# A decoder layer on one core: sums of tokens in portions one step apart, the first weight sums by DMA asked for later, and one load over ScalarE's queue

## The chip, the cores and the metric

The kernel runs on one core of one Trainium2 chip. The metric is the device time of one execution in microseconds (us). The kernel before took 818.30 us (median of three runs, 817.43 to 819.27).

## What is computed

One layer of a hybrid decoder on 256 tokens of width 2048, all in float32. Cut to what matters here:

```python
h = rmsnorm(x, norm_mix_g)
u = h @ w_in                       # 16384 columns: ten fields, the last two are ga and gb, 2048 wide each
ya = b_g * causal_dwconv3(c_g * xa) * silu(za)
yb = hgrn2(q, f, iv) normed per head * silu(og)
m = sigmoid(ga) * (ya @ w_a_out) + sigmoid(gb) * (yb @ w_b_out)
x = x + m @ w_o
x = x + sigmoid(rmsnorm(x) @ w_ple_gate) * (p @ w_ple_proj)
out = rmsnorm(x, final_norm_g)
```

## The kernel before

**One product in three.** Every float32 operand is cut into a high part, rounded to the type float32r, and the rest. A product is three matmuls, high by high, high by low and low by high (`triple`, L1030 to L1034); each has 128 tokens on the partitions and 512 columns. `cut` (L163) makes the two parts of a weight tile: ScalarE (ACT) copies to the high part (`whi`, L164) and VectorE (DVE) subtracts it (`wlo`, L165).

**Items and the loop.** The weights are walked in a list of items, one turn of the main loop (L1096) each. An item brings 256 rows by 512 columns: 1024 elements on each partition, 12 matmuls. At turn `pos` the loop cuts the item that lies three ahead (`ahead`, L1026) into one of four pairs of buffers, so its `whi` waits until TensorE has finished the item that used the pair before. Raw weights come over SyncE's queue (SP) in 1 MB loads of two items into three buffers.

**The part around the change.** `begun` is the last item of the gate ga of column group 0. I count from it and write b+1, b+2 and so on. b+1 to b+8 are gb of group 0, b+9 to b+12 `w_a` ("A0"), b+13 to b+16 `w_b` ("B0"). From b+17 on group 1 computes ga and gb together by a scheme of seven products in the place of eight, over tiles of 128 tokens by 128 rows. Its items are of two kinds: S items (slices c = 0, 2, 3, 5, 6) make seven products, 21 matmuls, named P1, c00, c10, P5, P7, P6, c01 in this order (`names_of`, L1049); slices 1, 4 and 7 are plain and are two C items each, 12 matmuls an item. So b+17 is S, b+18 and b+19 are C, b+20 and b+21 are S, b+22 and b+23 C, b+24 and b+25 S, b+26 and b+27 C; A1 and B1 follow. Groups 2 and 3 repeat this pattern.

**What an S item needs.** Sums of tokens: `token_sums` (L730) is a generator that makes them once, for all groups, in three portions (`TOGETHER`, L33: slice 0, slices 2 and 3, slices 5 and 6). A portion first rebuilds the tokens (`F`, in a buffer named `thi`, L744), then makes four sums (`S`, in `tlo`, L754), whose high part ACT writes to `shi` (L756) and whose low part DVE writes to `slo` (L757). Sums of weights: `add_by_dma` (L152) lets GpSimd's queue load one tile `sT` (L157) and, once that has landed, add a second one to it by an accumulating DMA (L158). `combine_weights` (L180) runs two turns ahead of the S item: two additions on DVE (L696, into `sA`) and three cuts, `sT` to `thi`/`tlo`, `sB` to `bhi`/`blo`, `sA` to `thi`/`tlo`. There are two buffers `sA` and two `sB`, loaded over SP (L141); the next load into one waits for the `tlo` or `blo` cut from it.

**What sets the order.** Generators in `active` are stepped once at the end of a turn, twice in S turns (L1174 to L1176). From `begun` to eight items past the start of A3 (`parked`) `pinned` (L1079) keeps ACT's and DVE's instructions in the order in which the code writes them; elsewhere a scheduler may reorder. TensorE's order is the scheduler's everywhere. Each engine works its queue in order, so an instruction that waits holds all behind it.

**Banks.** The products go to four PSUM banks `g` and four `s`. P6 and c01 of b+17 use the two banks that held B0's result; DVE frees them when it multiplies gb by that result (`ep_bb`, L776).

**The output projection.** O0 to O3 are `w_o`'s four column groups, eight items each. At O0's sixth item `third_part` (L996) opens the last pool and loads the first quarter of the residual x (`residual`, L983, two DMAs of 256 KB into `xs`), needed when O0 is done (`ep_o`, L816).

Of the kernel before, what the change touches and what calls it, by code (L numbers as in the profile page):

```python
# [47 lines left out]
def hybrid_kernel(ctx, tc, xT, x, pT, prm, gfin, masks, w_in, w_a, w_b, w_o, w_pg, w_pp, out):  # L48
    nc = tc.nc
# [11 lines left out]
    def open_pool(name, side):  # L61
        closers[name] = ExitStack()
        pools[name] = closers[name].enter_context(
            tc.tile_pool(name=name, bufs=1, side=side, reuse_waits="tile")
        )

    def close_pool(name):
        closers.pop(name).close()
        del pools[name]
# [3 lines left out]
    state = {"tmp": "tmp1"}  # L73
# [3 lines left out]
    def nm(s):  # L77
        uid[0] += 1
        return f"{s}_{uid[0]}"
# [5 lines left out]
    def bank(tag):  # L85
        return ps.tile([P, CW], F32, tag=tag, bufs=4, name=nm(tag))

    def sc(n, tag="sc", bufs=12):
        return small.tile([P, n], F32, tag=tag, bufs=bufs, name=nm(tag))
# [59 lines left out]
            else:  # L149
                nc.sync.dma_start(out=raw, in_=w[g, :, c : c + 2, :])  # L150

    def add_by_dma():  # L152
        pos = next((n for n, it in enumerate(items) if it["kind"] == "S" and n not in pair_sums), None)
        if pos is not None:
            w, g, c = items[pos]["w"]
            X = pair_sums[pos] = pools["st"].tile([P, 2, CW], F32, tag="sT", bufs=3, name=nm("sT"))
            nc.gpsimd.dma_start(out=X.rearrange("p n x -> p (n x)"), in_=w[g + 1, :, c, :])  # L157
            nc.gpsimd.dma_start(out=X, in_=w[g : g + 2, :, c, :CW].rearrange("n p x -> p n x"), accum_op=ALU.add)  # L158

    def pair_of(pool, n, tags=("whi", "wlo"), width=2 * CW):  # L160
        return tuple(pool.tile([P, width], F32R, tag=tag, bufs=n, name=nm(tag)) for tag in tags)
# [18 lines left out]
    def combine_weights(pos):  # L180
        st = pools["st"]
        (A, B), X = raw_of(pos), pair_sums[pos]
        add(A[:, 0], X[:, 0], B[:, 0])
        add(A[:, 1], A[:, 0], A[:, 1])
        ts = []
        for n, src in enumerate((X, B, A)):
            hi, lo = pair_of(st, 1, ("bhi", "blo"), CW) if n == 1 else pair_of(st, 3, ("thi", "tlo"))
            cut(hi, lo, src.rearrange("p n x -> p (n x)"))
            ts += [(hi[:, i * CW : (i + 1) * CW], lo[:, i * CW : (i + 1) * CW]) for i in range(1 if n == 1 else 2)]
        t1, t3, b22, t2, t4_ = ts  # L190
        sums[pos] = (b22, t1, t3, t2, t4_)
        add_by_dma()
# [4 lines left out]
    begun = next(n for n, it in enumerate(items) if it["kind"] == "ga" and it["last"])  # L197
# [532 lines left out]
    def token_sums():  # L730
        nu = len(SEVEN[1])
        state["S"] = pair_of(pools["st"], 1, ("shi", "slo"), nu * 4 * P)
        state["S"] = tuple(v.rearrange("p (u s t) -> p u s t", u=nu, s=4) for v in state["S"])
        for first, n in TOGETHER:
            for _ in range(3):
                yield
            F, S = (
                pools["st"].tile([P, 2 * CW], F32R, tag=tag, bufs=3, name=nm(tag))[:, : n * 4 * P].bitcast(F32)
                for tag in ("thi", "tlo")
            )  # L740
            c = SEVEN[1][first]
            hi, lo = (v[:, 2 * c : 2 * (c + n), :] for v in state["hT"])
            Fv = F.rearrange("p (k t) -> p k t", t=T)
            nc.vector.tensor_tensor(out=Fv, in0=hi.bitcast(F32), in1=lo.bitcast(F32), op=ALU.add)  # L744
            yield
            Fv = F.rearrange("p (u r b t) -> p u r b t", u=n, r=2, b=2)
            Sv = S.rearrange("p (u s t) -> p u s t", u=n, s=4)
            a11, a12, a21, a22 = Fv[:, :, 0, 0], Fv[:, :, 1, 0], Fv[:, :, 0, 1], Fv[:, :, 1, 1]
            s1, s2, s3, s4 = (Sv[:, :, i] for i in range(4))
            for out, u, v, op in (  # L750
                (s1, a21, a22, ALU.subtract), (s2, s1, a11, ALU.subtract),
                (s3, a11, a21, ALU.subtract), (s4, a12, s2, ALU.add),
            ):
                nc.vector.tensor_tensor(out=out, in0=u, in1=v, op=op)  # L754
            hi, lo = (v[:, first : first + n] for v in state["S"])
            nc.scalar.activation(out=hi, in_=Sv, func=AF.Copy)  # L756
            nc.vector.tensor_tensor(out=lo, in0=Sv, in1=hi.bitcast(F32), op=ALU.subtract)  # L757
            yield
# [217 lines left out]
    def second_part():  # L976

        close_pool("tmp1")
        open_pool("st", "left")
        open_pool("tmp2", "right")  # L980
        state["tmp"] = "tmp2"

    def residual(j):  # L983

        for t in range(NT):
            s = slice(j * CW, (j + 1) * CW)
            nc.sync.dma_start(out=state["x"][:, t, s], in_=x[:, t, s])

    def load_gfin():
        g = state["gfin"] = pools["tmp3"].tile([P, D], F32, name="gfin_t")  # L990
# [5 lines left out]
    def third_part():  # L996

        close_pool("tmp2")
        close_pool("branch")
        open_pool("tmp3", "right")  # L1000
        state["tmp"] = "tmp3"
        xs = pools["tmp3"].tile([P, NT, D], F32, name="xs")
        state["x"] = xs
        residual(0)
        state["ss2"] = sc(8, "ss2", 1)
        state["ss3"] = sc(12, "ss3", 1)
        nc.gpsimd.memset(state["ss3"].rearrange("p (t j) -> p t j", t=NT)[:, :, 5:6], EPS)
# [14 lines left out]
    def finish():  # L1022
        while active:
            advance()
# [71 lines left out]
    for pos, it in enumerate(items[:last_group]):  # L1096
        mark = len(nc.cur_bb.bb.instructions)
        kind, j, c, last = (it[n] for n in ("kind", "j", "c", "last"))
        _, _, w, g, opname = groups[it["gi"]]
# [60 lines left out]
        else:  # L1160
# [3 lines left out]
            for i in range(2):  # L1164
                k = 2 * c + i
                s = slice(i * CW, (i + 1) * CW)
# [10 lines left out]
        if pos == begun:  # L1177
            finish()
            second_part()
            active.append(token_sums())  # L1180
            for _ in range(3):
                add_by_dma()
        if kind == "O" and j == 0 and c == nch - 3:
            finish()
            third_part()
        if kind == "O" and j > 0 and c == 1:
            residual(j)
# [20 lines left out]
    for t, halves in ((0, (0, 1)), (1, (0,)), (1, (1,))):  # L1208
        bk, n = bank("g"), CW // 2
        for c in range(nlast):  # L1210
# [4 lines left out]
            for i in range(2):  # L1215
                k = 2 * c + i
                s = slice(i * CW + halves[0] * n, i * CW + (halves[-1] + 1) * n)
# [83 lines left out]
```

## Time and profile before

| | |
|---|---|
| median of three runs | 818.30 us |
| the profiled execution, its own time | 818.19 us |
| its span in the trace | 816.14 us |
| TensorE busy in the span | 804.2 us |
| DVE busy | 589.0 us |
| ACT busy | 459.1 us |
| mean granted TensorE clock | 0.997 |

The profile is one execution. Between its own time and the span lie 2.05 us that the trace doesn't show. All times of rows are us from the start of the span; a row of the timeline gives start, duration, engine, line, operation, tiles and, in brackets, the idle time ahead of it with what ended that. PE is TensorE. A steady stream of 512-column matmuls starts one every 0.227 us; the duration in a row (0.39) is longer because they overlap, so lost time shows in the distance between starts more than in idle time.

### The profile page before, as it was taken

The page shows a single profiled execution, that of the slowest core. Times are in us where ns is not written, and L with a number is a line of the kernel's source. Part 1 is how long each engine was busy: PE and PEld are TensorE (multiplying, and loading weights), DVE is VectorE, ACT ScalarE, POOL GpSimd, SP SyncE. Part 2 cuts the span into 40 slices and gives each one's busy share as a digit, 9 for nine tenths or more (in the row PEclk, how much of TensorE's full clock was granted, in tenths as well). Part 3 has the DMA queues.
Part 4 walks back from the last instruction along what each step waited for, and adds up shares of the span by engine and source line. Part 5 has one row for each costly group of instructions (what it writes and reads, how often), then busy time and mean ns, then how long its engine had stood idle before and what let it go on. Part 6 is the DMA issues. An engine that isn't in the chain of part 4 may idle for free.

```text
span 816.1 us, 10646 instructions
## 1 busy us (share of the span) xinstructions
PE 804.2 (99%) x4059; PEld 664.6 (81%) x4059; DVE 589.0 (72%) x745; ACT 459.1 (56%) x614; POOL 49.2 (6%) x57
## 2 busy tenths in 40 slices
PE   9999999999999999999999999999999999999995
PEld 6888888888888888888888778888888788888885
DVE  6746588767766498766778988987988756677932
ACT  7576476465555466455545556556554546575623
POOL 1000000001000000012000110110100000001210
PEclk9999999999999999999999999999999999999998
DMA  9988555647867555649975898998944887796702
GB/s 334 396 302 287 198 205 169 235 138 270 253 235 250 198 175 195 206 161 327 350 246 194 243 290 289 291 276 260 278 171 174 299 283 281 250 343 267 275 35 103
DMA packets 52659, 198.52 MB, mean 243 GB/s; under 512 B 6784, under 2 KB 16256, under 8 KB 37888
## 3 DMA queue, kind: packets, MB, share of 16 engines
q1 hardware_dynamic: 45792, 181.07, 63.1%
q0 software_dynamic: 6240, 15.73, 8.3%
q10 hardware_dynamic: 576, 1.05, 0.4%
q8 instruction: 31, 0.51, 0.3%
q14 instruction: 20, 0.16, 0.1%
HBM read 184.19 MB, written 13.63 MB: 242 GB/s over the span
## 4 chain that ended last, share of the span: by engine, by line
PE 85%; DVE 7%; issue 3%; DMA 3%; ACT 2%; POOLq 0%; POOL 0%; DVEq 0%; ACTq 0%
PE g L1033 26%; PE g L1034 26%; PE g L1032 26%; DVE wlo L165 3%; PE s L1033 2%; PE s L1034 2%; PE s L1032 2%; DMA sA<-in_w_in 1%; DMA raw<-in_w_pp 1%; DVE tlo L165 1%; ACT whi L164 1%; DMA raw<-in_w_o 1%; DVE sA L696 1%; PE s L479 1%; DVE back L303 0%
## 5 line engine op out<-in xcount | busy, mean ns | idle before, releaser
L165 DVE TENSOR_TENSOR wlo<-raw,whi 128x1024 fp32r<-128x1024 f32 (+1 forms) x264 | 319.6, 1227 | 157.9 <-ACT whi L164 155.9
L164 ACT ACTIVATE whi<-raw 128x1024 fp32r<-128x1024 f32 (+1 forms) x264 | 272.8, 1049 | 205.0 <-PE g L1034 168.8
L1033 PE MATMUL g<-wlo,xh 128*128 128x512 f32 (+1 forms) x738 | 283.9, 385 | 0.0
L1034 PE MATMUL g<-whi,xl 128*128 128x512 f32 (+1 forms) x738 | 283.6, 385 | 0.0
L1032 PE MATMUL g<-whi,xh 128*128 128x512 f32 (+1 forms) x738 | 283.5, 385 | 0.0
L1033 PEld LDWEIGHTS g<-wlo,xh 128*128 128x128 f32 x738 | 138.7, 188 | 27.7 <-DVE wlo L165 0.3
L1032 PEld LDWEIGHTS g<-whi,xh 128*128 128x128 f32 x738 | 138.7, 188 | 27.4
L1034 PEld LDWEIGHTS g<-whi,xl 128*128 128x128 f32 x738 | 138.7, 188 | 27.4
L1033 PE MATMUL g<-wlo,mh 128*128 128x512 f32 x128 | 49.9, 390 | 0.3 <-DVE wlo L165 0.3
L1032 PE MATMUL g<-whi,mh 128*128 128x512 f32 x128 | 49.7, 389 | 0.0
L1034 PE MATMUL g<-whi,ml 128*128 128x512 f32 x128 | 49.5, 389 | 0.0
L1033 PE MATMUL s<-wlo,xh 128*128 128x512 f32 x84 | 32.7, 390 | 0.0
L1034 PE MATMUL s<-whi,xl 128*128 128x512 f32 x84 | 32.7, 389 | 0.0
L1032 PE MATMUL s<-whi,xh 128*128 128x512 f32 x84 | 32.5, 390 | 0.0
L164 ACT ACTIVATE thi<-sA 128x1024 fp32r<-128x1024 f32 x15 | 15.9, 1062 | 27.6 <-DVE sA L696 24.7
L1033 PEld LDWEIGHTS g<-wlo,mh 128*128 128x128 f32 x128 | 24.0, 188 | 5.7 <-DVE wlo L165 0.7
L1032 PEld LDWEIGHTS g<-whi,mh 128*128 128x128 f32 x128 | 24.0, 188 | 5.1
L1034 PEld LDWEIGHTS g<-whi,ml 128*128 128x128 f32 x128 | 24.0, 188 | 4.9
L1034 PE MATMUL g<-whi,ybTl 128*128 128x512 f32 x64 | 24.9, 389 | 0.0
L1033 PE MATMUL g<-wlo,ybTh 128*128 128x512 f32 x64 | 24.9, 389 | 0.0
L1032 PE MATMUL g<-whi,yaTh 128*128 128x512 f32 x64 | 24.9, 389 | 0.0
L1033 PE MATMUL g<-wlo,yaTh 128*128 128x512 f32 x64 | 24.9, 389 | 0.0
(215 smaller groups left out, 908.4 us busy)
## 6 DMA issues: line engine op xcount, KB each, us to landing
raw<-in_w_in SPq DMA_DIRECT2D x66, 1024.0 KB, 5.0
raw<-in_w_o SPq DMA_DIRECT2D x16, 1024.0 KB, 6.1
raw<-in_w_pg SPq DMA_DIRECT2D x16, 1024.0 KB, 5.6
sT<-in_w_in POOLq DMA_DIRECT2D x30, 512.0 KB, 7.4
raw<-in_w_in SPq DMA_DIRECT2D x28, 512.0 KB, 6.6
raw<-in_w_a SPq DMA_DIRECT2D x8, 1024.0 KB, 6.8
raw<-in_w_b SPq DMA_DIRECT2D x8, 1024.0 KB, 6.7
turn<-t SPq DMA_DIRECT2D x60, 128.0 KB, 3.0
```

Of the source, the lines that this page charges most:

```text
L164: a = nc.scalar.activation(out=hi, in_=src, func=AF.Copy)
L165: v = nc.vector.tensor_tensor(out=lo, in0=src, in1=hi.bitcast(F32), op=ALU.subtract)
L479: nc.tensor.matmul(out, X[:, 0, h, s], X[:, 1, h, t], start=True, stop=True, tile_position=(0, i * n))
L696: nc.vector.tensor_tensor(out=out, in0=a, in1=b, op=ALU.add)
L1032: nc.tensor.matmul(psum, oh, hi, start=first, stop=False)
L1033: nc.tensor.matmul(psum, oh, lo, start=False, stop=False)
L1034: nc.tensor.matmul(psum, ol, hi, start=False, stop=last)
```

## The change

Three edits.

1. `token_sums` waits two steps once and then one step ahead of each portion, where it waited three steps ahead of each. The first portion stays where it was, the second moves up by two steps, the third by four.
2. The first three `add_by_dma` calls move from the end of turn `begun` to the turns b+3, b+5 and b+7. Each first DMA now waits for the last `whi` that was written by then. (Later calls, from `combine_weights`, are as before.)
3. `residual(0)` is issued on ScalarE's DMA queue and no longer on SP's.

```diff
-    def add_by_dma():
+    def add_by_dma(behind=None):
...
-            nc.gpsimd.dma_start(out=X.rearrange("p n x -> p (n x)"), in_=w[g + 1, :, c, :])
+            d = nc.gpsimd.dma_start(out=X.rearrange("p n x -> p (n x)"), in_=w[g + 1, :, c, :])
+            if behind is not None:
+                tc.add_manual_dep(
+                    d.ins, behind.name,
+                    mybir.DependencyInfo(mybir.DependencyClass.Sync, mybir.DependencyReason.DATA), reason="order",
+                )
...
+        yield
+        yield
         for first, n in TOGETHER:
-            for _ in range(3):
-                yield
+            yield
...
-    def residual(j):
+    def residual(j, queue=nc.sync):
...
-            nc.sync.dma_start(out=state["x"][:, t, s], in_=x[:, t, s])
+            queue.dma_start(out=state["x"][:, t, s], in_=x[:, t, s])
...
-        residual(0)
+        residual(0, nc.scalar)
...
-            for _ in range(3):
-                add_by_dma()
+        if pos in (begun + 3, begun + 5, begun + 7):
+            add_by_dma(state["splits"][0])
```

On DVE, at the first combination of weights (item b+17), the third portion stands in the middle before. `thi_3790<-xh,xl` is its F, the four rows `tlo_3791` its sums; `sA`, `tlo_3796`, `blo`, `tlo_3804` are the combination:

```order
L165 TENSOR_TENSOR wlo_3771<-sA_3701,whi_3770 128x1024
L744 TENSOR_TENSOR thi_3790<-xh_121,xl_122 128x1024
L696 TENSOR_TENSOR sA_3701<-sT_3500,sB_3702 128x512
L165 TENSOR_TENSOR tlo_3804<-sA_3701,thi_3803 128x1024
L165 TENSOR_TENSOR wlo_3811<-raw_3727,whi_3810 128x1024
L754 TENSOR_TENSOR tlo_3791<-thi_3790 128x2x128
L757 TENSOR_TENSOR slo_3531<-tlo_3791,shi_3530 128x1024
L165 TENSOR_TENSOR wlo_3836<-raw_3727,whi_3835 128x1024
L776 TENSOR_TENSOR gb_3661<-gb_3661,g_3752 128x512
```

(Rows of the same kind between these are left out.) Now the same engine has the portion (`thi_3711`, `tlo_3712`) among the cuts of B0, and the combination runs through to `gb`:

```order
L170 TENSOR_TENSOR wlo_3674<-raw_3576,whi_3673 128x1024
L170 TENSOR_TENSOR wlo_3692<-raw_3622,whi_3691 128x1024
L750 TENSOR_TENSOR thi_3711<-xh_121,xl_122 128x1024
L170 TENSOR_TENSOR wlo_3715<-raw_3622,whi_3714 128x1024
L760 TENSOR_TENSOR tlo_3712<-thi_3711 128x2x128
L763 TENSOR_TENSOR slo_3522<-tlo_3712,shi_3521 128x1024
L170 TENSOR_TENSOR wlo_3740<-raw_3662,whi_3739 128x1024
L770 TENSOR_TENSOR ga_3500<-ga_3500,g_3677 128x512
L170 TENSOR_TENSOR wlo_3758<-raw_3662,whi_3757 128x1024
L170 TENSOR_TENSOR wlo_3780<-sA_3707,whi_3779 128x1024
L170 TENSOR_TENSOR wlo_3817<-raw_3730,whi_3816 128x1024
L782 TENSOR_TENSOR gb_3670<-gb_3670,g_3761 128x512
```

F, four sums and `slo` moved up by some ten rows; what is cut, added and multiplied is the same.

On TensorE the scheduler writes b+17 differently. Before, behind P7 (`g_3868`) stand products of b+18 and b+19 and even of b+20 (`whi_3861`), and P6 (`g_3865`) comes after them:

```order
L1034 MATMUL g_3868<-thi_3795,slo_3531 128x512
L1032 MATMUL s_3870<-whi_3810,xh_121 128x512
L1032 MATMUL s_3871<-whi_3835,xh_121 128x512
L1032 MATMUL s_3869<-whi_3861,xh_121 128x512
L1033 MATMUL s_3871<-wlo_3836,xh_121 128x512
L1032 MATMUL g_3865<-thi_3803,shi_3530 128x512
```

Now P6 and c01 (`g_3866`) follow P7 directly:

```order
L1040 MATMUL g_3868<-thi_3801,slo_3522 128x512
L1038 MATMUL g_3865<-thi_3809,shi_3521 128x512
L1039 MATMUL g_3865<-tlo_3810,shi_3521 128x512
L1040 MATMUL g_3865<-thi_3809,slo_3522 128x512
L1038 MATMUL g_3866<-thi_3809,xh_121 128x512
L1038 MATMUL s_3870<-whi_3816,xh_121 128x512
```

The two banks of B0's result are so asked for earlier than before.

On ACT, around O0, `mh` is the high part of the last quarter of m, and `whi` cuts of `w_o` stand around it. The two DMAs for `xs` now stand behind `mh`:

```order
L169 ACTIVATE whi_5502<-raw_5418 128x1024
L775 ACTIVATE mh_5207<-back_5377 128x1024
L993 DMA xs<-in_x 128x512 x2
L169 ACTIVATE whi_5518<-raw_5452 128x1024
L169 ACTIVATE whi_5550<-raw_5452 128x1024
```

Before, the same rows followed one another without the DMAs, which stood on SP behind two loads of `w_o`. Behind that place the scheduler also puts a few loads of `xs` and the load of the final gain in another order among the loads of `w_o`.

## The prediction

> **What bounds the kernel now.** I read the busy times first, then busy time by stretches of 40 us, then TensorE's timeline where a stretch is short, then the chain of waits there.
>
> ```profile
> PE 804.2 (99%) x4059; PEld 664.6 (81%) x4059; DVE 589.0 (72%) x745; ACT 459.1 (56%) x614; POOL 49.2 (6%) x57
> ```
>
> TensorE is busy for 99% of the span, and the change takes none of its matmuls away. So only time in which TensorE starts nothing can be won. The stretches (busy time and count for each engine in the page's order, then granted clock, DMA share, GB/s) show where that is:
>
> ```profile
> 360.00:400.00 40.00, 40.00 (x177) 32.91 (x176) 28.00 (x48) 22.63 (x39) 7.97 (x7) 1.00 0.93 300
> 440.00:480.00 40.00, 38.84 (x169) 31.13 (x168) 36.45 (x44) 22.93 (x26) 5.92 (x7) 1.00 0.82 248
> 480.00:520.00 40.00, 40.00 (x178) 33.10 (x178) 34.92 (x41) 20.87 (x24) 5.31 (x6) 1.00 0.93 286
> ```
>
> Group 1's stretch, 440 to 480, has 169 matmuls where group 2's has 178: nine starts of 0.227 us, about 2.0 us lost, at a granted clock of 1.00 in both. TensorE's timeline names the holds. The longest:
>
> ```profile
> 476.13 0.39 PE L1032 MATMUL s<-bhi,shi 128*128 128x512 f32 x1
> 477.66 0.50 PE L1033 MATMUL s<-blo,shi 128*128 128x512 f32 x1 [1.14 <-DVE blo L165]
> 477.99 0.40 PE L1034 MATMUL s<-bhi,slo 128*128 128x512 f32 x1
> ```
>
> From 476.13 to 477.99 are two starts, in a steady stream 0.45, so 1.86 - 0.45 = **1.41 us** lost, waiting for `blo` of the combination for b+24. The two others in the stretch:
>
> ```profile
> 448.99 1.36 PE L1032 MATMUL s<-whi,xh 128*128 128x512 f32 x4
> 450.19 0.42 PE L1033 MATMUL s<-wlo,xh 128*128 128x512 f32 x1
> 450.45 0.40 PE L1034 MATMUL s<-whi,xl 128*128 128x512 f32 x1
> ```
>
> ```profile
> 461.16 1.05 PE L1032 MATMUL g<-thi,shi 128*128 128x512 f32 x3
> 462.05 0.40 PE L1033 MATMUL g<-tlo,shi 128*128 128x512 f32 x1
> ```
>
> 448.99 to 450.45 holds five starts: 1.46 - 1.14 = **0.32**. 461.16 to 462.05 holds three: 0.89 - 0.68 = **0.21**. One hold lies ahead of the stretch, one far behind it:
>
> ```profile
> 389.64 0.39 PE L1032 MATMUL g<-whi,xh 128*128 128x512 f32 x1
> 389.92 0.50 PE L1033 MATMUL g<-wlo,xh 128*128 128x512 f32 x1
> 390.26 0.40 PE L1034 MATMUL g<-whi,xl 128*128 128x512 f32 x1
> ```
>
> ```profile
> 648.27 0.61 PE L1032 MATMUL g<-whi,mh 128*128 128x512 f32 x2
> 649.16 0.50 PE L1033 MATMUL g<-wlo,mh 128*128 128x512 f32 x1 [0.28 <-DVE wlo L165]
> 649.50 0.40 PE L1034 MATMUL g<-whi,ml 128*128 128x512 f32 x1
> ```
>
> These lose 0.62 - 0.45 = **0.17** and 1.23 - 0.68 = **0.55**. What the change can reach is 1.41 + 0.32 + 0.21 + 0.17 = 2.11, and 0.55 more if the third edit acts on the last one.
>
> **Why they arise.** At 389 `wlo` is late since DVE stood still for a tile that comes back by DMA:
>
> ```profile
> 384.64 1.25 DVE L303 STREAM_TRANSPOSE t<-t 128x1024 f32<-128x1024 f32 x1 [2.71 <-DMA t<-turn]
> ```
>
> ```profile
> 367.55 1.87 POOL L157 DMA_DIRECT2D sT<-in_w_in  x3
> ```
>
> The three `sT` pairs (3 MB) are asked for at 367.55, and the stretch 360 to 400 above has a DMA share of 0.93. Past 440 the third portion of the token sums stands inside the first combination, ScalarE's row first, VectorE's after it:
>
> ```profile
> 446.60 1.06 ACT L756 ACTIVATE shi<-tlo 128x1024 fp32r<-128x1024 f32 x1 [3.46 <-DVE tlo L754]
> ```
>
> ```profile
> 445.03 0.41 DVE L754 TENSOR_TENSOR tlo<-thi 128x256 f32<-128x256 f32 x1
> ...
> 447.70 1.23 DVE L757 TENSOR_TENSOR slo<-tlo,shi 128x1024 fp32r<-128x1024 f32 x1 [1.12 <-ACT shi L756]
> ```
>
> `shi` waits 3.46 us, and two `whi` behind it with it: the hold at 449. The portion takes DVE from 445.03 to 447.70 + 1.14 = 448.84, and 1.14 more for its F ahead, 4.95 us, so DVE is that late at the next combinations too. That explains 461, and 476 through a load:
>
> ```profile
> 463.40 8.67 DMA sA<-in_w_in
> ```
>
> `sA` can be asked for only when the last `tlo` before it is cut, at 463.4; it lands 8.67 later, at 472.07, and the cuts and sums from it to `blo` end at 477.6.
>
> **Edit 1, the portions.** Nothing is removed or added; about 5 us of DVE and 1.06 of ScalarE move from 438 to 449 up to 420 to 435. I stepped both queues by hand in the new order, with the durations of these rows (a cut on DVE follows the one before it by 1.14):
>
> ```profile
> 421.09 1.23 DVE L165 TENSOR_TENSOR wlo<-raw,whi 128x1024 fp32r<-128x1024 f32 x1 [1.48 <-ACT whi L164]
> ```
>
> ```profile
> 421.99 1.37 ACT L327 ACTIVATE gb<-g,r1r 128x512 f32<-128x512 f32 x2 [0.93 <-PE g L1034]
> ```
>
> The second portion's sums come at 422.2 behind A0's third `wlo`, `shi` at 423.8. That puts `gb`'s two rows, 421.99 before, at 424.8 and the next `whi` at 426.0, its `wlo` at 427.1. The third portion's F is at 429.4, its sums at 431.7, `slo` at 434.3. The last two `wlo` of B0 are done at 436.6 and 439.0; counting twelve starts of 0.227 an item back from 444.23 (below), TensorE wants them at 438.8 and 441.5. So they are **2 us early, and cost nothing**. The `wlo` from `sA` that opens the combination starts at 439.0. From there the order is now the same as in group 2:
>
> ```profile
> 501.29 1.23 DVE L165 TENSOR_TENSOR wlo<-sA,whi 128x1024 fp32r<-128x1024 f32 x1 [1.29 <-ACT whi L164]
> ...
> 506.76 2.35 DVE L165 TENSOR_TENSOR wlo<-raw,whi 128x1024 fp32r<-128x1024 f32 x2
> 509.03 1.28 DVE L776 TENSOR_TENSOR gb<-gb,g 128x512 f32<-128x512 f32 x2
> ```
>
> From that `wlo` to the two last ones are 5.47, to `gb` 7.74. So the two `wlo` for which TensorE held at 449 come at 444.4 and 445.6, more than 3 us early, and `gb` at 446.7, its halves done at 447.4 and 448.0.
>
> What is late next is P6. TensorE starts b+17 at
>
> ```profile
> 444.23 0.39 PE L1032 MATMUL s<-whi,xh 128*128 128x512 f32 x1
> ```
>
> and now has P6 as the sixth product there, 15 starts on, at 447.6, and c01 at 448.3. They need the banks that the halves of `gb` free at 447.4 and 448.0. **The margin is 0.25 to 0.33 us**, less some 0.1 from DVE's end to TensorE's start; before, other products stood between. A hold here is bounded by 0 and 0.4 (if my steps are 0.5 off); I take 0.1.
>
> The next combinations then run without the lag. `sA` for b+24 can be asked for at some 460.2, not 463.4. With 8.67 it lands 3.2 earlier and `blo` ends at 474.4, while TensorE asks for it at 476.36 less the earlier holds, 475.7: 1.3 in hand. So 1.41, 0.32 and 0.21 go.
>
> **Edit 2, the weight sums.** As many DMAs, moved. The three pairs are asked for behind `whi` of b+6, b+8 and b+10, at about 408.5, 413 and 418. They are needed from 437 on, some 8 us apart, with 8.7 us of landing twice each: done at about 426, 431 and 436 for 437, 445 and 454. The wait is on GpSimd's queue, behind which only the next pair stands. The transfers at 367 to 392 get the room, so the hold of 0.17 at 389 goes (bounds 0 and 0.17; the row's cause is the transposed tile's DMA, so I take all). What they now run beside are the loads of `w_a`, priced under the rivals.
>
> **Edit 3, the residual.**
>
> ```profile
> 645.76 1.43 SPq L987 DMA_DIRECT2D xs<-in_x  x2
> ```
>
> ```profile
> 640.62 6.07 DMA raw<-in_w_o
> ```
>
> The hold at 648 hangs on the `w_o` load asked for at 640.62, which lands at 646.68; `whi` and `wlo` from it follow at once. On SP the two `xs` DMAs stand 5 us behind that load, so taking them off SP doesn't ask for it sooner: the 0.55 stays. On ScalarE they stand between `mh` and a `whi`:
>
> ```profile
> 650.29 1.06 ACT L769 ACTIVATE mh<-back 128x1024 fp32r<-128x1024 f32 x1 [0.77 <-DVE back L303]
> 651.81 1.06 ACT L164 ACTIVATE whi<-raw 128x1024 fp32r<-128x1024 f32 x1 [0.46 <-PE g L1034]
> ```
>
> ```profile
> L904 ACTq DMA_DIRECT2D out<-xs x2: 371/372/372, 800.8 to 811.6; - x2
> ```
>
> One issue on ScalarE is 0.37, two 0.74, less the 0.46 for which that `whi` waits anyway: it moves by 0.3 to 0.4. Items are cut three turns (8 us) ahead, so TensorE doesn't see it: 0, and 0.4 if that cover were gone. `xs` itself is first added at 657.2, 6 us after the issue.
>
> **The sum.** 2.11 - 0.1 = 2.0 us. Against the profiled 818.19 (span 816.14 and 2.05 around it) this gives **816.2**; the median of the runs is 0.11 above the profiled one.
>
> **Rivals.** *Late loads of `w_a` (slower).* They are asked for at
>
> ```profile
> 407.92 2.60 SPq L150 DMA_DIRECT2D raw<-in_w_a  x2
> ```
>
> (the second at 410.19) and landed, by the DMA issues of 407 to 425, in
>
> ```profile
> raw<-in_w_a SPq DMA_DIRECT2D x2, 1024.0 KB, 5.8
> ```
>
> at a time with little else. Now the first `sT` pair goes at 408.5. Loads beside the `sT` pairs, in 373 to 392, took (minimum, median, maximum, us)
>
> ```profile
> DMA to landing us min/median/max: 7.6/9.3/10.9
> ```
>
> At 9.3 the first lands at 417.2, its cuts go into the idle 1.48 ahead of 421.09, and nothing changes. At 10.9 it lands at 418.8: its `wlo` 419.9, the next 421.0, F of the second portion 422.2, A0's third `wlo` 423.3, a lag of 2.2 us. The portions fill the slack up to `gb`, so `gb` is 2.2 late and TensorE holds some 2.1 at P6: all of the gain, 818.2. Each further us of landing costs one; from 12.7 on the kernel is slower by over 0.2%, at 13 it takes some 818.2 + 2.1 = 820.3. For it: three loads in a row with the accumulating DMAs. Against: the moved pairs go one by one, five us apart, and the 10.9 had all three in flight.
>
> The page "DMA: Bandwidth & Descriptors" of the Trainium skill (Queues, rings and completion order) says that each of the 16 DMA engines takes the queue rows it has work for in turn, packet by packet. By equal turns 512 KB of `sT` would lengthen a 1 MB load by at most half of its 5.8 us, to an estimated 8.7, where the row with three pairs in flight has 10.9; by the page the lag is 0 and the forecast stands, by the row the gain is gone.
>
> *The margin at P6, or another long load.* At 0.3 to 1 us more lag on DVE than I stepped, P6 holds by as much; the `sA` load at 10.6 instead of 8.67 would bring back some 0.6 at 476. Either gives 816.7 to 817.5.
>
> *More than forecast.* If edit 3 also lets the 648 hold go: 815.5. Against: the row order above.
>
> *Nothing.* If the holds at 449, 461 and 476 come from elsewhere than the portions, 818.2.
>
> **How the numbers follow.** Forecast 0.45 (816.2), more 0.08, thin margin 0.24, nothing 0.11, slower 0.12. The range, 815.4 to 818.6, takes in 815.5 and the nothing case with the scatter of the runs and leaves out most of the slower rival. 0.2% is 1.64 us, about what a measurement of this kernel can tell from no change: the forecast and "more" are faster by over that (0.53), margin and nothing within it (0.35), the late loads slower (0.12).
>
> **What would show it.** Right: 178 matmuls in 440 to 480; no holds at 389, 449, 461 and 476; the one at 648 still there, 0.55; `shi` of the third portion near 433; `sA` for b+24 asked for at 460; the `w_a` loads landing in under 9.5 us; `xs` on ScalarE behind `mh` at 651 and the `whi` behind it 0.3 late. Wrong: P6 or c01 waiting for `gb` for over 0.4, `w_a` landing in over 10.5, or the `sA` load for b+24 in over 10.

## The result and the profile after

The changed kernel takes **815.89 us** (median of 22 runs, 814.66 to 819.44) against 818.23 before (median of 22): a ratio of **0.9976, 95% interval 0.9967 to 0.9985**, some 2.0 us less (1.2 to 2.7); the means of the 22 runs lie 1.98 apart, the medians 2.34. The forecast was 816.2. Its profiled execution took 816.50, with a span of 814.71, against 818.19 and 816.14.

The page's first line on the engines; TensorE is busy a microsecond less, the rest is as before:

```profile
PE 803.2 (99%) x4059; PEld 665.4 (82%) x4059; DVE 589.2 (72%) x745; ACT 459.4 (56%) x614; POOL 48.5 (6%) x57
```

Busy time in two of the stretches (columns as in the prediction: busy time and count of PE, PEld, DVE, ACT, POOL, then granted clock, DMA share, GB/s):

```profile
360.00:400.00 40.00, 40.00 (x179) 33.11 (x178) 28.82 (x49) 22.18 (x39) 2.54 (x1) 1.00 0.76 250
440.00:480.00 40.00, 38.95 (x173) 31.92 (x172) 34.97 (x40) 23.59 (x26) 7.11 (x8) 1.00 0.89 262
```

360 to 400 has lost its three weight sums (DMA share 0.76, it was 0.93), and 179 matmuls where there were 177. 440 to 480 has 173 matmuls, not 169, and not the 178 that I expected: one hold is still there. TensorE's timeline around it:

```profile
474.79 0.39 PE L1038 MATMUL s<-bhi,shi 128*128 128x512 f32 x1
476.23 0.50 PE L1039 MATMUL s<-blo,shi 128*128 128x512 f32 x1 [1.04 <-DVE blo L170]
476.56 0.40 PE L1040 MATMUL s<-bhi,slo 128*128 128x512 f32 x1
```

1.77 - 0.45 = 1.32 us, at the same `blo` as before. But the chain of waits that leads there is another one:

```profile
461.51 11.32 DMA sT<-in_w_in
472.83 0.03 issue
...
473.02 0.70 DVE sA L701
```

VectorE's own row says the same, with 4.48 us of idle time behind it:

```profile
473.02 0.69 DVE L701 TENSOR_TENSOR sA<-sT,sB 128x512 f32<-128x512 f32 x1 [4.48 <-DMA sT<-in_w_in]
```

Before, the combination waited for `sA`, asked for late because VectorE was late. Now VectorE is in time and `sA` is there (asked for at 459.65, landed at 463.65); what comes last is the accumulating DMA of the weight sum `sT`. It is the fifth pair, for the fifth S item, b+25 (the prediction called the item b+24; by the count of matmuls from 443.50 on it is b+25).

What the other steps look like after, VectorE first, then TensorE's P6 and c01:

```profile
445.85 1.28 DVE L782 TENSOR_TENSOR gb<-gb,g 128x512 f32<-128x512 f32 x2
```

```profile
446.90 0.39 PE L1038 MATMUL g<-thi,shi 128*128 128x512 f32 x1
447.13 0.39 PE L1039 MATMUL g<-tlo,shi 128*128 128x512 f32 x1
447.36 0.39 PE L1040 MATMUL g<-thi,slo 128*128 128x512 f32 x1
447.58 0.39 PE L1038 MATMUL g<-thi,xh 128*128 128x512 f32 x1
```

`gb`'s halves end at 446.5 and 447.1; P6 starts at 446.90 and c01 at 447.58, in the steady step of 0.227. The margins are 0.4 and 0.45. ScalarE's `shi` of the third portion has moved up, and the residual's DMAs stand behind `mh`:

```profile
432.42 1.06 ACT L762 ACTIVATE shi<-tlo 128x1024 fp32r<-128x1024 f32 x1 [3.91 <-DVE tlo L760]
```

```profile
648.88 1.07 ACT L775 ACTIVATE mh<-back 128x1024 fp32r<-128x1024 f32 x1 [0.78 <-DVE back L308]
648.88 0.82 ACTq L993 DMA_DIRECT2D xs<-in_x  x2
650.39 1.07 ACT L169 ACTIVATE whi<-raw 128x1024 fp32r<-128x1024 f32 x1 [0.45 <-PE g L1040]
```

### The profile page after: what moved, and what is told of

Same layout as the page of the kernel before. It is cut to its first block, busy times and chain, and to the rows that moved or that the text cites. A ratio compares the mean times of both kernels' runs of the same rounds, so it can differ in the third digit from the quotient of the medians.

```text
span 814.7 us, 10651 instructions
## 1 busy us (share of the span) xinstructions
PE 803.2 (99%) x4059; PEld 665.4 (82%) x4059; DVE 589.2 (72%) x745; ACT 459.4 (56%) x614; POOL 48.5 (6%) x57
## 4 chain that ended last, share of the span: by engine, by line
PE 85%; DVE 7%; issue 4%; DMA 2%; ACT 2%; POOL 0%; POOLq 0%; DVEq 0%; ACTq 0%
PE g L1038 26%; PE g L1039 26%; PE g L1040 25%; DVE wlo L170 3%; PE s L1039 2%; PE s L1040 2%; PE s L1038 2%; DMA sT<-in_w_in 1%; DMA raw<-in_w_o 1%; PE s L484 1%; DVE sA L701 1%; ACT whi L169 0%; DVE tlo L170 0%; PE s L932 0%; DVE back L308 0%
```

## Holds differ between executions

Each run below left a profile of one execution. This table sums, from TensorE's timeline of each, what the starts exceed the steady 0.227 at the five places of the prediction (us; "fifth pair" is when the fifth pair's accumulating DMA lands, "third pair" likewise; times from the span's start; in the three executions without edits 1 and 2 `sA` landed after the fifth pair):

| execution | edits | at 389 | at 449 | at 461 | at 476 | at 648 | third pair | fifth pair | span |
|---|---|---|---|---|---|---|---|---|---|
| before | none | 0.17 | 0.32 | 0.21 | 1.41 | 0.55 | 395.4 | 468.2 | 816.14 |
| before_again | none | 1.20 | 0.33 | 0.21 | 0.65 | 0.28 | 396.3 | 469.3 | 816.13 |
| e3_residual | 3 | 0.22 | 0.32 | 0.21 | 0.81 | 0.73 | 395.1 | 469.2 | 815.75 |
| e2_weight_sums | 2 | 0 | 0.32 | 0.21 | 1.07 | 0.64 | 445.2 | 473.2 | 815.14 |
| e1_portions | 1 | 0.66 | 0 | 0 | 0 | 0.29 | 395.4 | 469.2 | 813.70 |
| e13 | 1, 3 | 0.50 | 0 | 0 | 0 | 0.46 | 394.8 | 471.0 | 814.12 |
| after | 1, 2, 3 | 0 | 0 | 0 | 1.32 | 0.56 | 446.3 | 472.8 | 814.71 |
| after_again | 1, 2, 3 | 0 | 0 | 0 | 0.51 | 0.78 | 449.7 | 472.4 | 814.52 |
| e12 | 1, 2 | 0 | 0 | 0 | 0 | 0.84 | 445.8 | 470.7 | 813.48 |
| late | 1, 3, sums later | 0 | 0 | 0 | 1.22 | 0.70 | 446.2 | 472.7 | 814.72 |
| early | 1, 3, sums earlier | 0 | 0 | 0 | 0 | 0.41 | 435.0 | 468.1 | 813.16 |
| early_again | the same | 0 | 0 | 0 | 0 | 0.29 | 435.2 | 466.5 | 812.95 |
| at_once | 1, 3, sums together | 0 | 0 | 0 | 0 | 0.61 | 433.9 | 468.3 | 813.88 |

Two kinds of holds part here. Those at 449 and 461 come from the order on VectorE and ScalarE: 0.32 and 0.21 in every execution without edit 1, nothing with it. Those at 389, 476 and 648 wait for a DMA, and the same kernel shows 0.17 or 1.20, 1.41 or 0.65.

## The experiments

Each ratio below is against runs of the kernel before that were taken together with it (medians 817.75 to 818.08), so ratios compare better than times.

**Each edit alone**, and the changed kernel once more. The edits are the three parts of the diff above, taken one at a time.

> Edit 1 alone (the portions moved, the weight sums still asked for at begun, residual on SP). Theory A, that the gain is the holds of group 1 and edit 1 lifts them: 816.3 to 816.5 against 818.2 before, the holds at 449 and 461 gone, the one at 389 still there with 0.17. On the hold at 476, which the changed kernel's profile still shows with 1.3 us, two readings part. B: it is there because the moved sT pairs (edit 2) push the later pairs: then without edit 2 the fifth pair's accumulating DMA lands by 466 and no hold is left at 476. C: the combinations that now run earlier ask for their loads together, whatever edit 2 does: then the fifth pair still lands past 471 and a hold of 1 us or more stays, and the time is 817.5 or more.

Measured: 816.29 median, ratio 0.9979 (0.9970 to 0.9988). Its stretch 440 to 480 is full:

```profile
440.00:480.00 40.00, 40.00 (x178) 33.14 (x177) 37.82 (x42) 23.68 (x26) 5.92 (x7) 1.00 0.91 281
```

The fifth pair's two DMAs on GpSimd's queue, and VectorE's row that waited 4.48 in the changed kernel:

```profile
452.91 0.60 POOL L157 DMA_DIRECT2D sT<-in_w_in  x1 [4.01 <-DVE tlo L165]
458.99 1.17 POOL L158 DMA_DIRECT2D sT<-in_w_in  x1 [5.48 <-DMA sT<-in_w_in]
```

```profile
469.35 0.69 DVE L696 TENSOR_TENSOR sA<-sT,sB 128x512 f32<-128x512 f32 x1 [0.30 <-DMA sT<-in_w_in]
```

The first load lands within 6 us and the accumulating DMA follows at 458.99, 2.5 us earlier than in the changed kernel; it lands at 469.2, and VectorE waits 0.30. That is 3 us past the 466 that B named, and still in time for TensorE. So the cause that B names holds here and C doesn't: the earlier combinations alone bring no hold at 476. The time is the one of theory A. The hold at 389 was not 0.17 but 0.66:

```profile
388.94 0.39 PE L1033 MATMUL g<-whi,xh 128*128 128x512 f32 x1
389.72 0.50 PE L1034 MATMUL g<-wlo,xh 128*128 128x512 f32 x1 [0.39 <-DVE wlo L165]
390.06 0.40 PE L1035 MATMUL g<-whi,xl 128*128 128x512 f32 x1
```

> Edit 2 alone (the weight sums asked for at b+3, b+5, b+7; portions and residual as before). Theory A: only the hold at 389 goes, 0.17: 818.0. Theory B (edit 2 loads the queues past 440): the holds at 449 to 476 stay or grow, by up to 0.5 in sum, 818.0 to 818.7. A rival, that edit 2 carries the gain: 816.5 or less.

Measured: 816.84, ratio 0.9986 (0.9977 to 0.9996). The hold at 389 is gone, those at 449 and 461 stand, that at 476 is 1.07 with the fifth pair landing at 473.2: after edit 2 it is `sT` that comes last even without edit 1. None of the three forecasts has the time right: the gain is more than the 0.17 I gave it, somewhere in 0.3 to 1.9 us. The hold at 389, which the table has at 0.55 on average without this edit, lies within that.

> Edit 3 alone (the residual's first quarter asked for on ScalarE's queue). Theory A: nothing, 818.2 within 0.4, the hold at 648 as before with 0.55. Rival, that edit 3 carries a part of the gain: 817.5 or less and a shorter hold at 648.

Measured: 818.22, ratio 0.9998 (0.9989 to 1.0008), the hold at 648 0.73:

```profile
647.67 0.61 PE L1032 MATMUL g<-whi,mh 128*128 128x512 f32 x2
648.73 0.50 PE L1033 MATMUL g<-wlo,mh 128*128 128x512 f32 x1 [0.45 <-DVE wlo L165]
649.07 0.40 PE L1034 MATMUL g<-whi,ml 128*128 128x512 f32 x1
```

Nothing, as forecast.

> The changed kernel once more, for a second profile of it. If the hold at 476 is what this kernel does, its profile shows it again with 1 us or more and the fifth sT pair landing past 471. If it depends on the execution, the hold is shorter or absent here, and the execution's own time is lower by as much.

Measured: 815.77, ratio 0.9972 (0.9963 to 0.9981); the profiled execution took 816.30. The hold at 476 is 0.51, the fifth pair lands at 472.4. It belongs to this kernel, but its size depends on the execution. The execution's own time is only 0.2 lower, not by the 0.81 that this hold is shorter: it was 0.32 behind the first one at 135 us already and was held 0.22 longer at 648.

**The kernel before once more.**

> The kernel before once more, for a second profile: whether the holds at 389 (0.17 in the first) and 476 (1.41) are the same in another execution. If they follow the landing of DMAs, they differ by some tenths of a us; those at 449 and 461, which follow the order on VectorE and ScalarE, are 0.32 and 0.21 again within 0.05.

Measured: 817.90 in the profiled execution. The holds at 449 and 461 are 0.33 and 0.21; that at 476 is 0.65, less by 0.76, and that at 389 seven times what it was, so both moved by more than the tenths that I expected:

```profile
389.63 0.39 PE L1032 MATMUL g<-whi,xh 128*128 128x512 f32 x1
390.95 0.50 PE L1033 MATMUL g<-wlo,xh 128*128 128x512 f32 x1 [0.93 <-DVE wlo L165]
391.28 0.39 PE L1034 MATMUL g<-whi,xl 128*128 128x512 f32 x1
```

1.65 - 0.45 = 1.20. VectorE waited for the transposed tile by 3.74 here, and by 2.71 in the first profile:

```profile
385.66 1.25 DVE L303 STREAM_TRANSPOSE t<-t 128x1024 f32<-128x1024 f32 x1 [3.74 <-DMA t<-turn]
```

One us later from the DMA, one us more of TensorE's time.

**When the sums are asked for.**

```diff
-        if pos in (begun + 3, begun + 5, begun + 7):
+        if pos in (begun + 1, begun + 3, begun + 5):   # early, early_again
+        if pos in (begun + 5, begun + 7, begun + 9):   # late
+        if pos == begun + 3:                           # at_once: three calls
```

> The changed kernel with the three requests of weight sums two turns earlier (b+1, b+3, b+5). Theory B, that the moved pairs push the later ones over GpSimd's queue and the hold at 476 is their price: the third pair lands some 5 us earlier than in the changed kernel (446 to 450 there), the fifth pair's accumulating DMA by 470, the hold at 476 is 0.3 or less, no hold at 389: 815.2 to 815.5. Theory C, that the earlier combinations themselves bring the loads together: the hold at 476 stays at 0.5 to 1.3, and the time at 815.8 or above.

Measured: 815.40, ratio 0.9967 (0.9957 to 0.9978).

```profile
440.00:480.00 40.00, 40.00 (x178) 33.14 (x177) 37.79 (x43) 23.57 (x26) 5.91 (x7) 1.00 0.91 283
```

No hold at 389, none at 476. GpSimd's queue in the changed kernel, from the first pair's accumulating DMA on, and then in the early version, from the second pair's plain load on:

```profile
416.40 1.22 POOL L163 DMA_DIRECT2D sT<-in_w_in  x1 [8.03 <-DMA sT<-in_w_in]
417.16 1.07 POOL L157 DMA_DIRECT2D sT<-in_w_in  x1
428.05 1.19 POOL L163 DMA_DIRECT2D sT<-in_w_in  x1 [9.82 <-DMA sT<-in_w_in]
428.81 1.02 POOL L157 DMA_DIRECT2D sT<-in_w_in  x1
440.23 1.19 POOL L163 DMA_DIRECT2D sT<-in_w_in  x1 [10.39 <-DMA sT<-in_w_in]
442.23 0.59 POOL L157 DMA_DIRECT2D sT<-in_w_in  x1 [0.81 <-DVE tlo L170]
```

```profile
407.88 0.57 POOL L157 DMA_DIRECT2D sT<-in_w_in  x1 [1.40 <-ACT whi L169]
410.59 1.25 POOL L163 DMA_DIRECT2D sT<-in_w_in  x1 [2.13 <-DMA sT<-in_w_in]
416.20 1.19 POOL L163 DMA_DIRECT2D sT<-in_w_in  x1 [4.37 <-DMA sT<-in_w_in]
416.94 1.03 POOL L157 DMA_DIRECT2D sT<-in_w_in  x1
429.01 1.17 POOL L163 DMA_DIRECT2D sT<-in_w_in  x1 [11.04 <-DMA sT<-in_w_in]
442.23 0.60 POOL L157 DMA_DIRECT2D sT<-in_w_in  x1 [12.04 <-DVE tlo L170]
447.19 1.18 POOL L163 DMA_DIRECT2D sT<-in_w_in  x1 [4.37 <-DMA sT<-in_w_in]
```

L157 is a pair's plain load, L163 its accumulating DMA. In the changed kernel the queue waits 8 to 10 us at each L163 for the plain load ahead, and the next pair's L157 stands behind that wait. So the pairs follow one another at 12 us and the third may add only at 440.23, just when the fourth and the loads of the next combinations start. In the early version the third is out of the way by 435; the fourth's plain load then lands in 4.7 us, not in 7.3. The head start alone doesn't give this: the first pair is asked for 1.9 us earlier (405.72 and not 407.61), and the third is done 11.3 us earlier. The order on the queue differs too. In the early version the second pair's plain load (407.88) stands ahead of the first pair's accumulating DMA (410.59), and the two first waits are 2.13 and 4.37.

> The changed kernel with the three requests two turns later (b+5, b+7, b+9). Theory B: each pair waits on GpSimd's queue until the one before it may add, so the third pair lands at 455 or later where ScalarE wants it at 453, and the fourth and fifth land 5 us later than in the changed kernel (459 and 472): the combinations run late, TensorE holds 2 to 6 us in sum between 455 and 485, 818 to 822. Theory C: the later pairs don't follow the first three, and the time is within 0.5 of the changed kernel's 815.9.

Measured: 815.44, ratio 0.9978 (0.9969 to 0.9987). **This expectation of theory B was wrong.** The third pair did not come later than in the changed kernel (446.2): asked for at 412.4 and not 407.6, the first pair's plain load found the first load of `w_a` landed (411.92) and the second 2.4 us from it (414.81), and took 4.3 us, not 8.5. What was asked for 4.8 us later landed only 0.6 later. The time is within 0.5 of the changed kernel's, as theory C had it. The fifth pair is as late as in the changed kernel, and so is the hold:

```profile
472.85 0.69 DVE L701 TENSOR_TENSOR sA<-sT,sB 128x512 f32<-128x512 f32 x1 [4.15 <-DMA sT<-in_w_in]
```

> The changed kernel with all three pairs asked for at b+3, as many in flight as before the change, now beside the loads of w_a. The prediction's slower rival: these loads land in 9.3 to 10.9 and not in 5.1 to 7.5, VectorE is late by up to 2.2 at A0's third cut, and TensorE holds up to 2.1 at P6: 816 to 818. If instead the loads land in under 9, no hold at P6, and as the three pairs are then done by 437 the fifth pair is as early as with edit 1 alone: 815.3.

Measured: 815.50, ratio 0.9966 (0.9955 to 0.9977). Landing of the two `w_a` loads (minimum, median, maximum), in the changed kernel and in this one:

```profile
DMA to landing us min/median/max: 5.1/6.3/7.5
```

```profile
DMA to landing us min/median/max: 5.2/6.6/8.1
```

No hold at P6 in either: the rival of late `w_a` loads did not come true, even with the plain loads of three pairs in flight. (Their accumulating DMAs were first issued at 416.66, when the `w_a` loads had all but landed, the second at 417.53.) And with the third pair done at 433.9 there is no hold at 476. The first pair is asked for at 408.08 here, later than in the changed kernel, and the third is done 12.4 us earlier: all three plain loads stand ahead of the first accumulating DMA on the queue. So what counts is how many waits stand one behind another there, more than when the first pair is asked for.

> The version with requests two turns earlier once more. Theory B: again no hold at 389 and none above 0.1 at 476, and 815.2 to 815.5, 0.3 to 0.5 below the changed kernel. If its first profile was a lucky execution, a hold of 0.5 or more at 476 comes back and the time is that of the changed kernel.

Measured: 815.06, ratio 0.9961 (0.9949 to 0.9973), a little below the forecast, no hold at 389 and none at 476.

**One edit taken back from the three.**

> Edits 1 and 2 without edit 3 (the residual's first quarter on SP again). If edit 3 does nothing, this is the changed kernel: 815.8 within 0.5, no holds at 389, 449 and 461, one at 476 of 0.5 to 1.3 with the fifth pair landing past 472. If edit 3 carries part of the gain, 816.4 or more and a longer hold at 648.

Measured: 815.47, ratio 0.9969 (0.9957 to 0.9982). Not told apart from the changed kernel. Its profile has no hold at 476, where 0.5 to 1.3 was expected, although VectorE still waits for the fifth pair, which landed at 470.7:

```profile
470.93 0.69 DVE L701 TENSOR_TENSOR sA<-sT,sB 128x512 f32<-128x512 f32 x1 [2.63 <-DMA sT<-in_w_in]
```

From this add to the end of `blo` are 3.2 us, and TensorE asks for `blo` at about 475. So, as an estimate from these rows, landing by some 471.5 costs nothing and each us past it costs one. The landings in the table, 470.7 here and 472.4 and 472.8 in the two executions with all three edits, lie around this edge.

> Edits 1 and 3 without edit 2 (the weight sums asked for at begun, as before the change). Theory B: the third pair lands before 400, the fifth by 470, no hold at 476; a hold at 389 of 0.2 to 1.2 is back. 815.8 to 816.5. Theory C: a hold of 0.5 or more at 476 all the same.

Measured: 816.09, ratio 0.9977 (0.9968 to 0.9986), a hold of 0.50 at 389 and none at 476. B once more, C not; the fifth pair lands at 471.0, a little past the 470 that B named and still in time.

**The hold that no edit touches.** The turning of the parked m one turn earlier, in the early version:

```diff
                     nc.sync.dma_start(out=srcs[i], in_=state["m", i].rearrange("p a x -> p (a x)"))
                 yield
-                yield
```

> The early version, with one yield less ahead of the turning of the parked m, so that 7 us of VectorE's work around 616 to 633 is one turn earlier, into idle time at 608 and 611. The hold at 648 waits for a load that is asked for when VectorE, busy without a gap from 615 to 640, has freed a buffer. If that lag is its cause, the load is asked for up to 1.7 earlier and the hold of 0.3 to 0.8 goes: 814.7 to 815.1. If the load's landing alone decides it, the hold stays at 0.3 or more and the time is that of the early version, 815.4.

Measured: 815.37, ratio 0.9966 (0.9954 to 0.9978). The hold at 648 is gone and another of 0.29 is there at 624:

```profile
623.63 0.61 PE L1037 MATMUL g<-whi,ybTh 128*128 128x512 f32 x2
624.27 0.50 PE L1038 MATMUL g<-wlo,ybTh 128*128 128x512 f32 x1
624.61 0.40 PE L1039 MATMUL g<-whi,ybTl 128*128 128x512 f32 x1
```

The load on which 648 hangs is asked for at the same time, in the early version and in this one:

```profile
637.86 0.40 SPq L150 DMA_DIRECT2D raw<-in_w_o  x1
```

```profile
637.77 0.39 SPq L150 DMA_DIRECT2D raw<-in_w_o  x1
```

So the theory that this moves the load up is not borne out: VectorE's rows changed places, its idle 1.75 at 611 stayed, and the lag at 636 with it. The hold moved, and the time stayed that of the early version. None is left at 648 because the load landed 0.27 earlier here (643.47 and not 643.74) and TensorE, held at 624, came 0.29 later. What would ask for that load sooner stays open.

## Why the prediction was right, and where it was not

**The total was right, in part by luck; two of its terms were not.** The forecast gain was 2.0, and 2.0 was measured (1.2 to 2.7). But the holds, taken as averages over the profiles, give 1.43. That lies in the interval too; the agreement to a tenth is luck.

**Edit 1, the portions: right.** The hand-stepped queue gave `gb` at 446.7 in the time of before; after, b+17 starts at 443.50 and not 444.23, 0.73 earlier, and `gb` at 445.85: the step is right to 0.12. `sA` was asked for at 459.65, forecast 460.2. The holds of 0.32 and 0.21 are gone in all executions with edit 1 and stand in all without it. P6's thin margin held: 0 instead of 0.1.

**The hold of 1.41 at 476: the cause named was right, the term was mis-sized.** Edit 1 takes the late `sA` away; in e1_portions and e13 `sT` lands last, at 469.2 and 471.0, in time, and this hold is gone. But the step "the next combinations then run without the lag ... So 1.41, 0.32 and 0.21 go" looked at one load of that combination and not at its other one. With edit 2 `sT` lands later still, and of the three executions that carry edits 1 and 2 as made, one held 1.32, one 0.51, one nothing: on average 0.61, where before, before_again and e3_residual have 0.96. So edit 1 takes 0.96 away and edit 2 brings 0.61 back. The term is worth some 0.35 here, and 1.41 was the largest of its sizes.

**Edit 2: the step that failed is the schedule of the pairs.** "Done at about 426, 431 and 436" counted the second and third pair as overlapping, asked for at 413 and 418. They were asked for at 417.2 and 428.8, each behind a wait, and the three were done at 424.9, 437.6 and 446.3. The prediction said that only the next pair stands behind the wait on GpSimd's queue and did not draw the consequence. The page "DMA: Bandwidth & Descriptors" of the Trainium skill (Anatomy of one DMA, SWDGE path) has the rule: the DMA engines wait on no semaphore, any wait is on the issuing sequencer before dispatch. The trace agrees, with 8.03, 9.82 and 10.39 us of waiting ahead of the changed kernel's three L163 rows above. The slack to the use at 437, 445 and 453 hid this for the first three pairs; the fifth paid. So on top of edit 1 the second edit won 0.55 at 389 and lost 0.61 at 476, nothing in sum. The times agree: edit 1 alone is at 0.9979, edits 1 and 3 at 0.9977, not told apart from the 0.9976 and 0.9972 with all three.

**The hold of 0.17 at 389: right in cause, too small.** In the five executions without edit 2 it is 0.17, 1.20, 0.22, 0.66 and 0.50, 0.55 on average, and 0 in all with it. I took the size from one execution, of a hold that waits for a DMA. This error and the one at 476 have opposite signs: 0.32 + 0.21 + 0.55 + 0.35 = 1.43. The mean spans of before, before_again and e3 on one side and after, after_again and e12 on the other differ by 1.77; to the 1.43 come 0.43 that lie ahead of the 701st matmul, at some 135 us, where the kernels are the same, and the 648 hold takes 0.2 back; about 0.1 is left over. That the 0.43 are chance is likely, since at_once (135.15) and early (134.60) differ by as much, and the kernel with edit 1 alone has 134.51; but it was not shown.

**Edit 3: right.** Nothing at 648 (in the table 0.28 to 0.84 without this edit and 0.29 to 0.78 with it), and alone 0.9998. The `whi` behind the two issues waits 0.45, as before, and is not 0.3 late. The residual has less cover than I said, since its second DMA can take 9 us; VectorE waited for it in after_again, and TensorE held nowhere for that:

```profile
658.10 0.69 DVE L822 TENSOR_TENSOR xs<-xs,g 128x512 f32<-128x512 f32 x1 [1.84 <-DMA xs<-in_x]
```

**The rivals.** Late `w_a` loads: 7.5 at most after, 8.1 with three plain loads in flight, below the 9.3 up to which nothing changes. The estimate of at most 8.7, worked out from the Trainium skill's rule that each DMA engine takes its queue rows in turn (the same page, Queues, rings and completion order), was the better one for these loads. The row with 10.9 came from a stretch in which the accumulating DMAs of the pairs were in flight; at_once had only the plain loads beside `w_a`, so three accumulating DMAs beside these loads were not tried. The margin case "another long load" was the right suspicion with the wrong load: `sT`, not `sA`.

**A better version.** With the sums asked for two turns earlier the holds at 389 and 476 are both gone: 0.9967 and 0.9961 in two measurements, against 0.9976 and 0.9972 of the changed kernel. The intervals overlap, so the times alone don't tell these kernels apart by the some 0.8 us between them; the profiles have 0.61 of it at 476.

## What to carry to other kernels

A hold that ends on a DMA has no fixed size: take its cause from one profile, and its price from several executions, or as a range. When a lag is taken away, look at every operand of the instruction that was late; the next one in time is the new bound. And a queue that waits for one transfer before it may ask for the next sets a pace of its own: count the waits that stand one behind another on it. Here asking 4.8 us later at its head left its end where it was, and putting the plain loads ahead of the first wait moved it by 12 us.

## What was not expected of the hardware

A DMA asked for 4.8 us later can land only 0.6 later: the first pair's plain load of 512 KB took 8.5 us from 407.6, beside two 1 MB loads, and 4.3 from 412.4. And DMAs of one size on one queue differ by a factor of three: the quickest plain loads of 512 KB in these executions took 4.05 to 4.7 us, the fifth pair's accumulating DMA 6.9 to 11.7, and the plain load that follows it on the queue 8.9 to 13.4. Since that plain load is slow too, the runs don't show that adding is what takes the time.
